# Two fused transformer blocks on one core: new places in SBUF for the matmul operands, and value projections 512 columns wide

## Chip, cores and metric

One core of a Trainium2 chip runs the whole program in one launch. The metric is device microseconds (us) of that core, the median of three runs.

## What is computed

A sequence of 256 tokens with 1,024 features passes a first block (two layers, each a mixer and a squared-ReLU MLP) and a second block (a gated recurrence beside an attention, then a gated FFN). Cut to its skeleton:

```python
def first_block(x, ...):
    for i in range(2):
        hn = rms_norm(x, norm_mix[i])
        mix = even_mixer(hn, ...) if i % 2 == 0 else odd_mixer(hn, ...)
        x = x + mix
        x = x + square(relu(rms_norm(x, norm_mlp[i]) @ w1[i])) @ w2[i]
    return rms_norm(x, norm_final)

def odd_mixer(hn, w_in, w_out, bias_table):
    q, k, v = split(hn @ w_in, 3)
    return moba_attention(q, k, v, bias) @ w_out

def second_block(x, ...):
    xa, ga, q, k, v, f, g_a, g_b = split(rms_norm(x) @ w_in)
    y_a = gelu(ga) * rg_lru(conv(xa)); y_b = forgetting_attention(q, k, v, f)
    x = x + rms_norm((sigmoid(g_a) * (y_a @ w_a) + sigmoid(g_b) * (y_b @ w_b)) @ w_out)
    return x + rms_norm((gelu(gate) * val) @ w_down)      # gate, val = conv(rms_norm(x) @ w_up)
```

All data are 32-bit. The second layer's `v` and the second block's `v` are the two value projections that the change touches (1,024 x 1,024 each).

## The kernel before

Activations stand feature-major: `x`, `gh`, `gl` are tiles of 128 partitions x 8 feature tiles x 256 tokens. For precision every product of an activation with a weight is three products of rounded 32-bit parts: the activation is split into `gh` (rounded) and `gl` (the rest), a weight into `whi` and `wlo`, and `mm3` (L262 to L264) issues whi x gh, whi x gl, wlo x gh into one PSUM bank. Each has a weight load of 128 columns (LDWEIGHTS) and a moving operand of 256 tokens; the load of one matmul runs beside the matmul before it. The same three lines work on other moving tiles:

- `hh`, `hl`: the MLP's hidden features (32 tiles; `hh2`, `hl2` with 24 in the FFN), the "down" stages
- `yh`, `yl`: the recurrence's output
- `oh`, `ol`: the attention's output (`oh1` in the second layer, `oh2` in the second block)

Weights come as a stream (the list `chunks`, `w_load`, `w_split`): a DMA from SyncE brings 1 MB into one of three `raw` buffers, and for each half of it (a unit: 8 x 128, 4 x 256 or 5 x 128 columns) ScalarE casts 128 x 1,024 into `whi` (L220) and VectorE subtracts into `wlo` (L221). There are six buffers of each, and `w_next` keeps up to four units split ahead of TensorE. The program's order is written by hand: generators (`gen_pair`, `gen_nat`, `gen_deep`, `gen_half`) issue a few matmuls at a time, and `Pend.step` and `tick` issue the evacuations in between; `weave` interleaves them with the steps of an attention or of the recurrence.

The value projections are the one place where the roles are turned: `gen_nat` (L435 to L437) makes the activation the loaded operand, and the weights (256 columns of a unit) the moving one, so that the values come out token-major. It takes two units, goes through the eight feature tiles for the first 128 tokens, then for the other 128, and `evac_nat` (L844) scales two halves of 256 columns into `vn`. It is called with n = 4 for the second layer and the second block, and with n = 1 three times in the first layer.

Tiles have no given addresses. Each pool hands out its tiles in the order in which they are asked for, and pools lie one behind the other, so a tile's place follows from the sizes of those ahead of it. In the built program the places (byte within a partition, rest after division by 512) are those of the table in the section on the change. All steps from one feature tile to the next are 512 or 1,024 bytes, so in these stages every matmul of a stage has the same rest for its moving operand and the same for its weights. Two products of the first projections are the exception: the gate logits of the first layer (24 columns) and the forget logits of the second block (16 columns), `gen_small`, whose loaded weights are packed at steps of 96 and 64 bytes.

Of the kernel before, what the change touches and what calls it, by code (L numbers as in the profile page):

```python
# [58 lines left out]
def kernel(  # L59
# [31 lines left out]
    np_ = ctx.enter_context(tc.tile_pool(name="np", bufs=2))  # L91
    rawp = ctx.enter_context(tc.tile_pool(name="rawp", bufs=3))
# [38 lines left out]
    U4 = [(4, 256), (4, 256)]  # L131
    U5 = [(5, 128), (5, 128)]
# [17 lines left out]
    for i in range(4):  # L150
        chunks.append((w_od[i], UA, False))
# [9 lines left out]
    for i in range(10, 14):  # L161
        chunks.append((w_in2[i], UA, False))
# [9 lines left out]

    W = Ctl()
# [56 lines left out]
    # orders of k for a start on two pairs at once: unit by unit for a few k, or k by k  # L230
# [66 lines left out]
    class Norm:  # L297
        # sums of squares over the features; the last `tail` tiles go straight to the summing products
# [263 lines left out]
    def maps_gen(maps, ap):  # L562
# [5 lines left out]
        def A(n):  # L568
            if n % 2 == 0:
                # two heads side by side, on the upper and the lower rows of the array  # L570
                qs = []
                for i in (n, n + 1):
                    m = maps[i]
                    if m.get("pre"):
                        m["pre"]()
                    st[i] = pss.tile([128, 512], F32, tag="s", name="s")
                    qs.append((st[i], m["q"](), m["k"]()))
                for s, q, k in qs:
                    nc.tensor.matmul(out=s[:, 128:384], lhsT=q[:, 128:256], rhs=k, start=True, stop=True)  # L579
# [12 lines left out]
            st[n] = [p, sm, nm]  # L592
# [102 lines left out]
    tb_t = cp.tile([33, 16], F32, name="tb_t")  # L695
# [3 lines left out]
    warm = cp.tile([128, 8], F32, name="warm")  # L699
    nc.scalar.activation(out=warm, in_=mhalf, func=AF.Square)  # L700
    # the tensor engine's clock rises with use: keep it busy until the first weights are here
# [98 lines left out]
    wcmp = [ap0.tile([128, 2048], F32, tag="e8", name="wcmp%d" % i, bufs=2) for i in range(2)]  # L800
# [93 lines left out]
    def compress_gen():  # L894
# [17 lines left out]
        # keys on rows 0..29, values on rows 64..93  # L912
# [38 lines left out]
    # position n of the head order (i, g) -> head g * 4 + i  # L951
# [128 lines left out]
    # the first sums of squares, in tiles that are free so far  # L1080
# [9 lines left out]
    sgain = cp.tile([128, 1], F32, name="sgain")  # L1090
# [60 lines left out]
    def mlp(norm, gain_next, nrm, nrm2=None):  # L1151
        st = ExitStack()
        hp = st.enter_context(tc.tile_pool(name="hp", bufs=1))
        hh = hp.tile([128, 32, T], FR, name="hh")
# [15 lines left out]
    mlp(norm, lambda j: V("mix1", j), nrm)  # L1170
    norm = nrm

    def log1pe(pool, z, n, pre):
        # log(1 + exp(-|z|)) by 2 atanh(e / (2 + e)); returns the steps and the result
# [29 lines left out]
    A1 = ExitStack()  # L1204
    ap1 = A1.enter_context(tc.tile_pool(name="a1", bufs=1))
    rb8 = ap1.tile([128, T], F32, name="rb8")
    vn = ap1.tile([128, 2, D], F32, name="vn")
    oh = ap1.tile([128, KT, T], FR, name="oh1")
    ol = ap1.tile([128, KT, T], FR, name="ol1")
# [11 lines left out]
    def evac_v1(j, ps):  # L1221
        if j == 0:
            nc.vector.tensor_scalar(out=rb8, in0=norm.rb, scalar1=0.125, scalar2=None, op0=ALU.mult)
        evac_nat(vn)(j, ps)
# [30 lines left out]
    run(gen_nat(4, gh, gl, evac_v1, pend))  # L1255
# [12 lines left out]
    nsp = cp.tile([128, 10], F32, name="nsp")  # L1268
    psp = cp.tile([128, 10], F32, name="psp")
    hb = cp.tile([128, 20], F32, name="hb")  # L1270
    hm = cp.tile([128, 16], F32, name="hm")
# [21 lines left out]
    gc = cp.tile([128, 8], F32, name="gc")  # L1293
    nc.vector.tensor_tensor(out=gc, in0=V("fin"), in1=V("pre2"), op=ALU.mult)
    nA, nB = Norm(), Norm()
    mlp(norm, lambda j: gc[:, j:j + 1], nA, nB)

    M = ExitStack()
    mp = M.enter_context(tc.tile_pool(name="mp", bufs=1))
    yh = mp.tile([128, 10, T], FR, name="yh")  # L1300
# [98 lines left out]
    def rg_gen():  # L1399
        for half in range(2):  # L1400
# [5 lines left out]
            for o in range(5):  # L1406
# [3 lines left out]
                for m in range(2):  # L1410
                    # blocks off the diagonal reach at most half of the columns
# [33 lines left out]
    def evac_f(ps):  # L1445
# [14 lines left out]
        def st15():  # L1460
            # log_sigmoid(z) = min(z, 0) - log(1 + exp(-|z|))
# [12 lines left out]
    def evac_gate2(dst, hof):  # L1474
# [12 lines left out]
        gen_nat(4, gh, gl, evac_nat(vn), pend),  # L1487
# [236 lines left out]
def _nats(cols):  # L1724
# [3 lines left out]
    return [[(0, 4, cols[i:i + 256]), (4, 4, cols[i:i + 256])] for i in range(0, len(cols), 256)]  # L1728

# [57 lines left out]
def _prepare(I):  # L1787
# [77 lines left out]
    groups = _nats(ar(2048, 3072))  # L1865
# [8 lines left out]
    groups += _nats(ar(ov, ov + 1024))  # L1874
# [53 lines left out]
```

## Time and profile before

| | before |
|---|---|
| median of three runs | 1175.63 us (1173.75 to 1175.65) |
| profiled execution, first to last instruction (span) | 1170.4 us |
| around the span (median less span) | 5.2 us |
| TensorE matmul busy | 1138.5 us, 97% of the span |
| VectorE, ScalarE, GpSimd busy | 793.4, 625.7, 190.3 us |
| mean granted TensorE clock | 0.993 of 2.4 GHz |

PE is the matmul, PEld the weight load beside it, DVE VectorE, ACT ScalarE, POOL GpSimd. The profiled execution is known by its span; its own time is taken as the span and the 5.2 us around it. Matmuls overlap in the pipeline and each record is some 0.28 us long, so a matmul's duration is not its price: the price is the pace, the time from one start to the next. It is read from a stretch in which TensorE never rests, as its length divided by its matmuls; two that began just ahead of the stretch are counted in it and are taken off.

### The profile page before, as it was taken

How to read it: one execution, taken by the hardware profiler on the slowest of the kernel's cores; microseconds unless marked ns; L12 is line 12 of the kernel's file. 1: busy time of each engine (PE TensorE's matmuls, PEld its weight loads, DVE VectorE, ACT ScalarE, POOL GpSimd, SP SyncE). 2: the span in 40 equal slices, each digit the busy share in tenths (PEclk: the TensorE clock that was granted, in tenths of full speed). 3: DMA queues.
4: the chain of work that ended last, by engine and by line, in shares of the span. 5: the costliest groups of instructions: out<-in, count | busy, mean ns of one | idle time of the engine just before them, and what ended most of it. 6: DMA issues, size and time to landing. Idle time of an engine off the chain costs nothing.

```text
span 1170.4 us, 22694 instructions
## 1 busy us (share of the span) xinstructions
PE 1138.5 (97%) x9343; PEld 1088.1 (93%) x9343; DVE 793.4 (68%) x1404; ACT 625.7 (53%) x1112; POOL 190.3 (16%) x228
## 2 busy tenths in 40 slices
PE   8999999999999999999999999999999999999996
PEld 7987799999999889999999897999999999999996
DVE  5767766674545777566445787766567689999842
ACT  4346555653444545565434577644454556676641
POOL 2014320000010123000001000042310123222211
PEclk9999999999999999999999999999999989999998
DMA  8832244555444334355455453564555525445641
GB/s 331 290 136 73 74 180 145 212 202 199 177 184 180 141 113 145 144 214 206 158 215 198 153 204 109 175 239 141 166 180 197 173 99 167 164 175 180 212 149 36
DMA packets 31303, 200.01 MB, mean 171 GB/s; under 512 B 3594, under 2 KB 6042, under 8 KB 9056
## 3 DMA queue, kind: packets, MB, share of 16 engines
q1 hardware_dynamic: 28832, 187.23, 44.6%
q0 software_dynamic: 2080, 11.08, 2.9%
q8 instruction: 73, 1.20, 0.4%
q14 instruction: 30, 0.25, 0.1%
q10 hardware_dynamic: 288, 0.26, 0.1%
HBM read 197.43 MB, written 3.22 MB: 171 GB/s over the span
## 4 chain that ended last, share of the span: by engine, by line
PE 78%; DVE 14%; ACT 3%; issue 2%; POOL 2%; DMA 1%; SPq 0%; POOLq 0%; ACTq 0%
PE g L262 22%; PE g L264 21%; PE g L263 21%; DVE y L1643 4%; DVE wlo L221 4%; PE rgp L1414 2%; PE g L435 2%; PE g L436 2%; PE g L437 2%; PE pt L623 1%; PE o L673 1%; DVE u L1631 1%; ACT whi L220 1%; PE s L579 1%; DVE y L1655 1%
## 5 line engine op out<-in xcount | busy, mean ns | idle before, releaser
L221 DVE TENSOR_TENSOR wlo<-raw,whi 128x1024 fp32r<-128x1024 f32 (+2 forms) x356 | 420.3, 1212 | 114.2 <-ACT whi L220 113.9
L262 PE MATMUL g<-gh,whi 128*128 128x256 f32 x1632 | 463.7, 284 | 3.2 <-ACT whi L220 1.7
L264 PE MATMUL g<-gh,wlo 128*128 128x256 f32 x1632 | 460.1, 282 | 3.1 <-DVE wlo L221 3.1
L263 PE MATMUL g<-gl,whi 128*128 128x256 f32 x1632 | 457.6, 280 | 0.5 <-DVE gl L257 0.4
L220 ACT CAST whi<-raw 128x1024 fp32r<-128x1024 f32 (+2 forms) x356 | 349.9, 1024 | 18.0 <-PE g L263 8.4
L262 PEld LDWEIGHTS g<-gh,whi 128*128 128x128 f32 x1632 | 309.1, 189 | 10.6 <-issue 5.4
L264 PEld LDWEIGHTS g<-gh,wlo 128*128 128x128 f32 x1632 | 309.2, 189 | 7.2 <-DVE wlo L221 7.1
L263 PEld LDWEIGHTS g<-gl,whi 128*128 128x128 f32 x1632 | 309.4, 190 | 1.1 <-DVE gl L257 0.7
L262 PE MATMUL g<-hh,whi 128*128 128x256 f32 x704 | 199.4, 283 | 1.3 <-DVE u L1631 1.3
L264 PE MATMUL g<-hh,wlo 128*128 128x256 f32 x704 | 199.3, 283 | 0.2 <-DVE wlo L221 0.2
L263 PE MATMUL g<-hl,whi 128*128 128x256 f32 x704 | 199.2, 283 | 0.0
L262 PEld LDWEIGHTS g<-hh,whi 128*128 128x128 f32 x704 | 135.1, 192 | 1.5 <-ACT q L1652 1.5
L264 PEld LDWEIGHTS g<-hh,wlo 128*128 128x128 f32 x704 | 135.1, 192 | 0.4 <-DVE wlo L221 0.4
L263 PEld LDWEIGHTS g<-hl,whi 128*128 128x128 f32 x704 | 135.1, 192 | 0.0
L317 POOL TENSOR_TENSOR acc<-acc,sq 128x256 f32<-128x256 f32 x53 | 42.4, 806 | 465.2 <-ACT sq L313 464.3
L612 POOL TENSOR_TENSOR p<-p,rr 128x384 f32<-128x384 f32 x56 | 50.1, 895 | 205.9 <-DVE rr L607 92.8
L597 ACT ACTIVATE p<-p,nm 128x256 f32<-128x256 f32 x112 | 49.9, 448 | 56.0 <-DVE nm L588 55.8
L1643 DVE SCALAR_TENSOR_TENSOR y<-u,cw,y 128x255 f32<-128x255 f32 (+1 forms) x96 | 60.1, 685 | 0.0
L262 PE MATMUL g<-oh,whi 128*128 128x256 f32 x192 | 55.6, 290 | 0.0
L264 PE MATMUL g<-oh,wlo 128*128 128x256 f32 x192 | 54.3, 283 | 0.0
L263 PE MATMUL g<-ol,whi 128*128 128x256 f32 x192 | 54.2, 282 | 0.0
L1160 ACT ACTIVATE u<-u 128x512 f32<-128x512 f32 x32 | 20.2, 632 | 61.9 <-DVE u L1159 61.9
(317 smaller groups left out, 1455.8 us busy)
## 6 DMA issues: line engine op xcount, KB each, us to landing
raw<-in_w_in_dram SPq DMA_DIRECT2D x30, 1024.0 KB, 4.9
raw<-in_w_up_dram SPq DMA_DIRECT2D x24, 1024.0 KB, 4.9
raw<-in_w_m1a_dram SPq DMA_DIRECT2D x16, 1024.0 KB, 4.8
raw<-in_w_m2a_dram SPq DMA_DIRECT2D x16, 1024.0 KB, 5.0
raw<-in_w_m1b_dram SPq DMA_DIRECT2D x16, 1024.0 KB, 4.9
raw<-in_w_m2b_dram SPq DMA_DIRECT2D x16, 1024.0 KB, 4.9
raw<-in_w_od_dram SPq DMA_DIRECT2D x12, 1024.0 KB, 4.8
raw<-in_w_dn_dram SPq DMA_DIRECT2D x12, 1024.0 KB, 4.8
```

The source lines that it names most:

```text
L220: nc.scalar.copy(out=hi[:, a:b], in_=t[:, off + a:off + b])
L221: nc.vector.tensor_tensor(out=lo[:, a:b], in0=t[:, off + a:off + b], in1=hi[:, a:b].bitcast(F32), op=ALU.subtract)
L262: nc.tensor.matmul(out=o, lhsT=wh, rhs=xh, start=start, stop=False, skip_group_check=skip)
L263: nc.tensor.matmul(out=o, lhsT=wh, rhs=xl, start=False, stop=False, skip_group_check=skip)
L264: nc.tensor.matmul(out=o, lhsT=wl, rhs=xh, start=False, stop=stop, skip_group_check=skip)
L317: nc.gpsimd.tensor_tensor(out=self.acc, in0=self.acc, in1=dst, op=ALU.add)
L435: nc.tensor.matmul(out=ps[:, b, :], lhsT=xh[:, k, bs], rhs=wh[:, k % 4, :], start=(k == 0), stop=False)
L436: nc.tensor.matmul(out=ps[:, b, :], lhsT=xh[:, k, bs], rhs=wl[:, k % 4, :], start=False, stop=False)
L437: nc.tensor.matmul(out=ps[:, b, :], lhsT=xl[:, k, bs], rhs=wh[:, k % 4, :], start=False, stop=(k == KT - 1))
L597: nc.scalar.activation(out=p[:, c0:c1], in_=p[:, c0:c1], func=AF.Exp, scale=-1.0, bias=nm[:, b:b + 1], accum_out=sm[:, b:b + 1],)
L612: nc.gpsimd.tensor_tensor(out=pv, in0=pv, in1=w, op=ALU.mult)
L1643: nc.vector.scalar_tensor_tensor(out=y[:, a, d:], in0=u[:, a, 0:T - d], scalar=cw[:, w, c:c + 1], in1=y[:, a, d:], op0=ALU.mult, op1=ALU.add)
```

## The change

Unwritten pad tiles are put at the head of pools (sizes in 4-byte words), `wcmp` and the attention outputs move to the head of theirs, and the small tiles of `cp` are asked for at the start, so that the operands of the matmuls come to other places. No instruction is added by that.

| tile | bytes behind a multiple of 512, before | after | moving tile less weights, before | after |
|---|---|---|---|---|
| `whi`, `wlo` (six each) | 320 | 0 | | |
| `gh`, `gl` | 384 | 192 | 64 | 192 |
| `hh`, `hl` of the first MLP | 320 | 160 | 0 | 160 |
| `hh`, `hl` of the second MLP | 320 | 224 | 0 | 224 |
| `hh2`, `hl2` of the FFN | 320 | 96 | 0 | 96 |
| `yh`, `yl` | 320 | 192 | 0 | 192 |
| `oh`, `ol`, first layer | 416 | 192 | 96 | 192 |
| `oh1`, `ol1`, second layer | 320 | 32 | 0 | 32 |
| `oh2`, `ol2`, second block | 320 | 64 | 0 | 64 |
| `raw` (three) | 64 | 384 | | |

The second part: the two value projections with n = 4 become `gen_wide` with n = 2. A unit is now 2 feature tiles x 512 columns, a matmul moves 512 columns into a whole PSUM bank, both halves of the tokens take each unit in turn, and the evacuation is 512 wide.

```diff
+    pad(xp, 32)
     x = xp.tile([128, KT, T], F32, name="x")
+    pad(xp, 48)
     gh = xp.tile([128, KT, T], FR, name="gh")
...
+    U2 = [(2, 512), (2, 512)]
...
-        chunks.append((w_od[i], UA, False))
+        chunks.append((w_od[i], U2, False))
...
+    pad(wp, 96)
     W = Ctl()
...
+    def gen_wide(n, xh, xl, evac, pend):
+
+        for j in range(n):
+            pss_ = [psg.tile([128, 2, T], F32, tag="g", name="g") for _ in range(2)]
+            for u in range(4):
+                wh, wl, (nk, ncol) = w_next()
+                for b in range(2):
+                    bs = slice(b * 128, b * 128 + 128)
+                    o = pss_[b].rearrange("p a t -> p (a t)")
+                    for k in range(2):
+                        kk = 2 * u + k
+                        nc.tensor.matmul(out=o, lhsT=xh[:, kk, bs], rhs=wh[:, k, :], start=(kk == 0), stop=False)
+                        nc.tensor.matmul(out=o, lhsT=xh[:, kk, bs], rhs=wl[:, k, :], start=False, stop=False)
+                        nc.tensor.matmul(out=o, lhsT=xl[:, kk, bs], rhs=wh[:, k, :], start=False, stop=(kk == KT - 1))
+                    if u == 3:
+                        pend.put(lambda j=j, b=b, o=o: evac(j, b, o))
+                    pend.step()
+                    yield
...
+    def evac_wide(dst):
+        def f(j, b, ps):
+            c = j * 512
+            nc.scalar.activation(out=dst[:, b, c:c + 512], in_=ps, func=AF.Copy, scale=norm.rn[:, b:b + 1])
+        return f
...
+    def mlp(norm, gain_next, nrm, nrm2=None, place=48):
...
+        pad(hp, place)
         hh = hp.tile([128, 32, T], FR, name="hh")
...
-    run(gen_nat(4, gh, gl, evac_v1, pend))
+    run(gen_wide(2, gh, gl, evac_v1, pend))
...
+    pad(mp, 48)
     yh = mp.tile([128, 10, T], FR, name="yh")
...
-        gen_nat(4, gh, gl, evac_nat(vn), pend),
+        gen_wide(2, gh, gl, evac_wide(vn), pend),
...
+    pad(ff, 24)
     hh = ff.tile([128, 24, T], FR, name="hh2")
```

The order of the instructions moves only around the two value projections. On TensorE, at the start of the second layer's projection (`g` is the PSUM bank, the numbers tell buffers apart, the last field is the output's size), before:

```order
2447 L264 MATMUL g_3854<-hh_1954,wlo_3856 128x256
2448 L435 MATMUL g_3995<-whi_3885,gh_91 128x256
2449 L436 MATMUL g_3995<-wlo_3886,gh_91 128x256
2450 L437 MATMUL g_3995<-whi_3885,gl_92 128x256
2469 L435 MATMUL g_3995<-whi_3913,gh_91 128x256
2472 L435 MATMUL g_3995<-whi_3885,gh_91 128x256
```

and now:

```order
2447 L282 MATMUL g_3864<-hh_1964,wlo_3866 128x256
2448 L475 MATMUL g_4002<-whi_3895,gh_101 128x512
2449 L476 MATMUL g_4002<-wlo_3896,gh_101 128x512
2450 L477 MATMUL g_4002<-whi_3895,gl_102 128x512
2454 L475 MATMUL g_4003<-whi_3895,gh_101 128x512
2460 L475 MATMUL g_4002<-whi_3923,gh_101 128x512
```

Before, both units of a step were held through all eight feature tiles and one bank; now a unit is used up in twelve matmuls on two banks, and then the next is taken. The program has 8,484 matmuls in place of 8,676. On ScalarE at the same place (casts of units, then the broadcast of the norm, then the evacuations), before:

```order
188 L220 CAST whi<-raw 128x1024 x3
189 L356 ACTIVATE dg<-cs,rn 128x128
190 L364 COPY rb<-nbc 128x256
191 L844 ACTIVATE vn<-g,rn 128x256 x4
192 L220 CAST whi<-raw 128x1024 x2
193 L844 ACTIVATE vn<-g,rn 128x256 x2
```

and now:

```order
188 L238 CAST whi<-raw 128x1024 x2
189 L374 ACTIVATE dg<-cs,rn 128x128
190 L382 COPY rb<-nbc 128x256
191 L238 CAST whi<-raw 128x1024
192 L886 ACTIVATE vn<-g,rn 128x512 x2
193 L238 CAST whi<-raw 128x1024 x4
```

Eight evacuations of 256 columns have become four of 512, in two groups, and a cast stands between the norm's broadcast and the first of them.

## Rows read from the trace of the kernel before

**Rows 1.** The page: busy time by engine, and the chain by engine.

```profile
PE 1138.5 (97%) x9343; PEld 1088.1 (93%) x9343; DVE 793.4 (68%) x1404; ACT 625.7 (53%) x1112; POOL 190.3 (16%) x228
PE 78%; DVE 14%; ACT 3%; issue 2%; POOL 2%; DMA 1%; SPq 0%; POOLq 0%; ACTq 0%
```

**Rows 2.** Stretches inside stages: length, busy time and instructions of each engine.

```profile
core 0: us, PE busy (x) PEld busy (x) DVE busy (x) ACT busy (x) POOL busy (x), PEclk, DMA share, GB/s
184.00:244.00 60.00, 60.00 (x532) 60.00 (x531) 40.91 (x46) 36.27 (x47) 0.00 (x0) 1.00 0.58 204
482.00:545.00 63.00, 63.00 (x538) 63.00 (x537) 43.33 (x48) 37.86 (x48) 0.00 (x0) 1.00 0.56 200
748.00:781.00 33.00, 33.00 (x282) 33.00 (x281) 22.35 (x28) 16.35 (x23) 13.12 (x13) 1.00 0.70 240
246.00:337.00 91.00, 91.00 (x761) 91.00 (x760) 46.90 (x50) 38.32 (x49) 4.45 (x6) 1.00 0.54 199
546.50:637.50 91.00, 91.00 (x761) 91.00 (x760) 45.37 (x49) 41.11 (x56) 8.66 (x12) 1.00 0.52 195
1096.00:1152.00 56.00, 56.00 (x470) 56.00 (x468) 26.18 (x25) 24.99 (x38) 8.22 (x10) 1.00 0.42 151
143.00:155.00 12.00, 12.00 (x103) 12.00 (x102) 9.40 (x14) 7.45 (x13) 0.00 (x0) 1.00 0.48 176
887.60:910.40 22.80, 22.80 (x192) 22.80 (x192) 19.28 (x29) 11.23 (x15) 0.00 (x0) 1.00 0.57 209
```

**Rows 3.** Groups of TensorE by line and shape: count, busy us, mean ns, idle before.

```profile
L263 PE MATMUL g<-gl,whi 128*128 128x256 f32 x1632 | 457.6, 280 | 0.5 <-DVE gl L257 0.4
L263 PE MATMUL g<-hl,whi 128*128 128x256 f32 x704 | 199.2, 283 | 0.0
L263 PE MATMUL g<-ol,whi 128*128 128x256 f32 x192 | 54.2, 282 | 0.0
L263 PE MATMUL g<-yl,whi 128*128 128x256 f32 x80 | 22.6, 282 | 0.0
L437 PE MATMUL g<-whi,gl 128*128 128x256 f32 x176 | 49.2, 280 | 0.0
```

**Rows 4.** Timeline of PE in the 16-column product (start, us), then one load.

```profile
713.39 0.28 PE L264 MATMUL gs<-gh,wlo 128*16 128x256 f32 x1
...
714.52 0.28 PE L262 MATMUL gs<-gh,whi 128*16 128x256 f32 x1
714.52 0.09 PEld L263 LDWEIGHTS gs<-gl,whi 128*16 128x16 f32 x1
```

**Rows 5.** Stretches of two pairs of the FFN's "up" stage.

```profile
1002.10:1008.20 6.10, 5.93 (x50) 5.72 (x50) 6.10 (x11) 4.22 (x7) 1.68 (x2) 1.00 0.49 169
1020.40:1026.50 6.10, 5.72 (x50) 5.52 (x50) 6.10 (x11) 4.22 (x7) 1.68 (x2) 1.00 0.52 176
```

**Rows 6.** A value projection: a stretch of it, and ScalarE's evacuations by shape.

```profile
347.00:360.50 13.50, 13.50 (x117) 13.50 (x117) 5.02 (x5) 6.33 (x11) 0.00 (x0) 1.00 0.31 109
L844 ACT ACTIVATE vn<-g,rn 128x256 f32<-128x256 f32 x8 | 3.4, 473 | 7.6 <-PE g L437 7.6
L1160 ACT ACTIVATE u<-u 128x512 f32<-128x512 f32 x32 | 20.2, 632 | 61.9 <-DVE u L1159 61.9
```

**Rows 7.** What TensorE waited for: us in total, times, longest.

```profile
PE pt L623 <- POOL p L612: 5.4, 7, 1.3
PE g L264 <- DVE wlo L221: 3.3, 18, 0.4
```

**Rows 8.** DMA issues of the weight stream: KB each, median us to landing.

```profile
raw<-in_w_m1a_dram SPq DMA_DIRECT2D x16, 1024.0 KB, 4.8
raw<-in_w_m2a_dram SPq DMA_DIRECT2D x16, 1024.0 KB, 5.0
```

More of the change, by code (lines that the diff above doesn't have):

```diff
@@ L91, with pad @@
     np_ = ctx.enter_context(tc.tile_pool(name="np", bufs=2))
+    pads = []
+    def pad(pool, n):
+        pads.append(0)
+        pool.tile([128, n], F32, tag="pad%d" % len(pads), name="pad", bufs=1)
     rawp = ctx.enter_context(tc.tile_pool(name="rawp", bufs=3))
@@ L103 @@
     mhalf = cp.tile([128, 8], F32, name="mhalf")
+    tb_t = cp.tile([33, 16], F32, name="tb_t")
+    warm = cp.tile([128, 8], F32, name="warm")
+    sgain = cp.tile([128, 1], F32, name="sgain")
+    nsp = cp.tile([128, 10], F32, name="nsp")
+    psp = cp.tile([128, 10], F32, name="psp")
+    hb = cp.tile([128, 20], F32, name="hb")
+    hm = cp.tile([128, 16], F32, name="hm")
+    gc = cp.tile([128, 8], F32, name="gc")
+    pad(xp, 32)
     x = xp.tile([128, KT, T], F32, name="x")
+    pad(xp, 48)
     gh = xp.tile([128, KT, T], FR, name="gh")
@@ L161 @@
     for i in range(10, 14):
-        chunks.append((w_in2[i], UA, False))
+        chunks.append((w_in2[i], U2, False))
     for i in range(14, 26):
@@ L694 @@
     w_load()
-    tb_t = cp.tile([33, 16], F32, name="tb_t")
     nc.vector.memset(tb_t[32:33, :], NEGB)
@@ L698 @@
     nc.vector.memset(mhalf, -0.5)
-    warm = cp.tile([128, 8], F32, name="warm")
     nc.scalar.activation(out=warm, in_=mhalf, func=AF.Square)
@@ L782 @@
     ap0 = A0.enter_context(tc.tile_pool(name="a0", bufs=1))
+    pad(ap0, 48)
+    wcmp = [ap0.tile([128, 2048], F32, tag="e8", name="wcmp%d" % i, bufs=2) for i in range(2)]
     qT = ap0.tile([128, 4, T], F32, name="qT")
@@ L799 @@
     nlam = ap0.tile([128, 1], F32, name="nlam")
-    wcmp = [ap0.tile([128, 2048], F32, tag="e8", name="wcmp%d" % i, bufs=2) for i in range(2)]
     for i in range(2):
@@ L1089 @@
     norm.tail = 3
-    sgain = cp.tile([128, 1], F32, name="sgain")
     have = {}
@@ L1147 @@
     A0.close()
-    def mlp(norm, gain_next, nrm, nrm2=None):
+    def mlp(norm, gain_next, nrm, nrm2=None, place=48):
         st = ExitStack()
         hp = st.enter_context(tc.tile_pool(name="hp", bufs=1))
+        pad(hp, place)
         hh = hp.tile([128, 32, T], FR, name="hh")
@@ L1169 @@
     nrm = Norm()
-    mlp(norm, lambda j: V("mix1", j), nrm)
+    mlp(norm, lambda j: V("mix1", j), nrm, place=40)
     norm = nrm
@@ L1205 @@
     ap1 = A1.enter_context(tc.tile_pool(name="a1", bufs=1))
+    pad(ap1, 8)
+    oh = ap1.tile([128, KT, T], FR, name="oh1")
+    ol = ap1.tile([128, KT, T], FR, name="ol1")
     rb8 = ap1.tile([128, T], F32, name="rb8")
     vn = ap1.tile([128, 2, D], F32, name="vn")
-    oh = ap1.tile([128, KT, T], FR, name="oh1")
-    ol = ap1.tile([128, KT, T], FR, name="ol1")
     qk = {}
@@ L1219, in evac_qk, with evac_v1 @@
         return f
-    def evac_v1(j, ps):
-        if j == 0:
+    def evac_v1(j, b, ps):
+        if j == 0 and b == 0:
             nc.vector.tensor_scalar(out=rb8, in0=norm.rb, scalar1=0.125, scalar2=None, op0=ALU.mult)
-        evac_nat(vn)(j, ps)
+        evac_wide(vn)(j, b, ps)
     def head4_maps(ap, j, bias, qk, vn, oh, ol, hdone):
@@ L1267 @@
     )
[L1268 to L1271, printed above, removed]
     sp_steps, sp_q = log1pe(cp, V("lam"), 10, "sp")
@@ L1290 @@
     bias_ctx.close()
-    gc = cp.tile([128, 8], F32, name="gc")
     nc.vector.tensor_tensor(out=gc, in0=V("fin"), in1=V("pre2"), op=ALU.mult)
     nA, nB = Norm(), Norm()
-    mlp(norm, lambda j: gc[:, j:j + 1], nA, nB)
+    mlp(norm, lambda j: gc[:, j:j + 1], nA, nB, place=56)
     M = ExitStack()
     mp = M.enter_context(tc.tile_pool(name="mp", bufs=1))
+    pad(mp, 48)
     yh = mp.tile([128, 10, T], FR, name="yh")
@@ L1498 @@
     fp = FA.enter_context(tc.tile_pool(name="fp", bufs=1))
+    pad(fp, 96)
     oh = fp.tile([128, KT, T], FR, name="oh2")
@@ L1728, in _nats, with _wides @@
     return [[(0, 4, cols[i:i + 256]), (4, 4, cols[i:i + 256])] for i in range(0, len(cols), 256)]
+def _wides(cols):
+    import numpy as np
+    cols = np.asarray(cols)
+    return [[(k, 2, cols[i:i + 512]), (k + 2, 2, cols[i:i + 512])] for i in range(0, len(cols), 512) for k in (0, 4)]
 def _deep(w, group=1):
@@ L1864, in _prepare @@
     w = I["od_w_in"][0]
-    groups = _nats(ar(2048, 3072))
+    groups = _wides(ar(2048, 3072))
     for j in range(4):
@@ L1873, in _prepare @@
     groups = _pairs(w, oxa, oxa + 1280) + _pairs(w, oga, oga + 1280)
-    groups += _nats(ar(ov, ov + 1024))
+    groups += _wides(ar(ov, ov + 1024))
     groups += _pairs(w, oa, oa + 1024)
```

## The prediction

> **What bounds the kernel now.** The page comes first: TensorE is busy for 97% of the span, and 78% of the chain that ended last is TensorE, 14% VectorE [rows 1]. So the pace of TensorE is the time, except where VectorE holds the chain. The list of waits agrees: the longest sum for which TensorE waited on another engine is 5.4 us, in the attentions, the next 3.3 us [rows 7].
>
> Then the stretches inside stages. All are of matmuls with 128 loaded columns and 256 moving ones, at granted clock 1.00 (the 2.4 GHz level), with TensorE never idle; yet the pace differs. With the two matmuls that reach in taken off:
> - first MLP, "up" (`gh`, gap 64 between moving tile and weights): 60.00 / 530 = 113.2 ns
> - second MLP, "up" (the same tile, the same gap): 63.00 / 536 = 117.5 ns; second block's gates and q, k: 33.00 / 280 = 117.9 ns
> - both "down" stages (`hh`, gap 0): 91.00 / 759 = 119.9 ns, twice; the FFN's: 56.00 / 468 = 119.7 ns
> - first layer's output projection (`oh`, gap 96): 12.00 / 101 = 118.8 ns; second block's (gap 0): 22.80 / 190 = 120.0 ns [rows 2].
>
> The clock, the shape and the instructions are the same, the places are not. The mean of one record tells the same: 280 ns with `gl`, 283 with `hl`, 282 with `ol` and `yl` [rows 3]. Gap 0 always gives 120; gap 64 gives 113 or 117.5, which it keeps for a whole stage. So there are two sorts of cost: one by place, and one by how the stream happened to start.
>
> How low can the pace go? In the product with 16 loaded columns a load lasts 0.09 us and hardly overlaps anything, its places run through gaps from 320 down to 128, and ten starts lie between 713.39 and 714.52: 113 ns [rows 4]. I take 113.2 as the floor for 256 moving columns, wherever the weights lie.
>
> One stage is not TensorE's. In the FFN's "up" stage VectorE is busy 6.10 of 6.10 us for a pair of units, TensorE 5.93 [rows 5]. The second pair shown is the test: TensorE needs only 5.72 there, and the pair takes 6.10 all the same.
>
> **The change, part by part.** The profiled execution has a span of 1170.4 us, 5.2 us under the median of 1175.6; terms are in us of span, and the 5.2 stays.
>
> *`gh` and `gl`, gap 64 to 192.* 3 x 1632 = 4896 matmuls [rows 3], of which 24 pairs x 48 = 1152 are the FFN's "up" stage; there VectorE's 6.10 stays and I cost them at nothing. If that cover were gone (VectorE shorter than 48 x 117.5 ns = 5.64 us) they would count 1152 x 4.3 ns = 5.0. Of the other 3744 no row has gap 192 with full loads. Bounds: 113.2 (the lowest row) and 120.0 (the highest). I take 113.2: the short loads ran at it over gaps on both sides of 192 [rows 4], while the known bad gap is 0. Then the second MLP gives 768 x 4.3 = 3.3; the second block's gates, q and k 576 x 4.7 = 2.7; the first MLP only some 0.7, since three quarters of it stand at 113.2 already; the other 1632, some at either pace, 1632 x 2.7 (taken a little above half of 4.5) = 4.4. Together 11.1.
>
> *`hh` of the two MLPs, gap 0 to 160 and 224.* 1536 matmuls at 119.9. Bounds 113.2 and 120.0 again. These places are no multiples of 64 bytes, and the one tile before that was none either (`oh`, at 416, gap 96) ran at 118.8, nearer to the upper end; but gap 96 is also nearer to 0. I take the middle: 1536 x 3.35 = 5.1.
>
> *`hh2` of the FFN, gap 0 to 96.* The row with gap 96 has 118.8 ± 1.2, one matmul more or less in its window, against 119.7 now: nothing.
>
> *The smaller tiles.* `yh` 0 to 192: 240 x 6.7 = 1.6. First `oh` 96 to 192: 192 x 5.6 = 1.1. `oh1` 0 to 32, the middle: 192 x 3.35 = 0.6. `oh2` 0 to 64, the paces of gap 64, of which 117.5 is the commoner: 192 x 2.5 = 0.5. Together 3.8.
>
> *Values 512 wide.* Away go 384 matmuls at 13.50 / 115 = 117.4 ns [rows 6], 45.1; in come 192. If what lies above 256 columns at 2.4 GHz (106.7 ns) is paid by the instruction, one takes 213.3 + 6.5 = 219.8 ns, all 42.2; if by the column, 226.4 at the floor, 43.5, or 240 at the worst pace, 46.1. I take 43.5, the floor by the column, which lies between: a gain of 1.6, bounds +2.9 and -1.0. Half of the weight loads go too, which run beside the matmuls. The evacuation: 8 x 473 ns = 3.8 of ScalarE becomes 4 x 632 = 2.5 [rows 6], and ScalarE is busy for 6.33 of 13.50 there: off the path. Banks: each round takes two of three, so the second half of the next round needs the first bank free; it has six matmuls of the old round and six of the new, 12 x 226 ns = 2.7, to be read in 0.63, with a cast of about 1 us perhaps ahead. No new wait. As many `Pend.step` calls (16) come at the same spacing, so the norm and the recurrence woven in come as before; a unit is used up in 12 x 226 ns = 2.7 where two took 5.6, so the weight stream keeps its rate.
>
> *Feeding it.* At 113.2 ns 1 MB is used up every 48 x 113.2 = 5.4 us; it lands in 4.8 to 5.0 with three buffers [rows 8], and the stretch from 184 to 244 ran like that without a gap, VectorE at 40.91 and ScalarE at 36.27 of 60 [rows 2]. The new place of `raw` and the pads are costed at nothing: no instruction comes with them.
>
> *What does not arrive.* In the two attentions of the first block and the `yh` stage TensorE waits for others now and then [rows 7]. Their share of the above is 1.1 + 1.1 (first layer, 408 `gh` matmuls), 1.0 + 0.6 (second, 384) and 1.6, 5.4 in all; I take a third as lost, 1.8.
>
> **Sum:** 11.1 + 5.1 + 3.8 + 1.6 - 1.8 = 19.8. Span 1150.6, time **1155.8 us**.
>
> **A rule against it.** Stages that differ in place, not in shape, clock or engine, run at 113.2, 117.5 and 119.9 [rows 2]. The Trainium skill, page SBUF — State Buffer, section "Who interferes with whom", gives TensorE two read ports, one for the moving operand and one for LDWEIGHTS, independent of each other, and says that TensorE never waits on anyone there. By it no place is better than another, and what is left of the sum is the 1.6 of the wide values: 1174. The trace does not bear it out as it stands, since three paces are seen; but two of them at one and the same place show that place is not everything.
>
> **The rivals.**
> - *Places do nothing by themselves* (the case beside that rule): the pace is a matter of how each stage's stream starts, and gap 0 was 120 by chance in every "down" stage. For: 113.2 and 117.5 at gap 64. Against: four stages at gap 0, all within 0.3 ns. Only the wide values count: 1174, 1172.7 to 1176.6. Also the case in which the new gaps win as much as they lose.
> - *All gaps but 0 are free.* `hh` gives its other half (5.1), `hh2` 576 x 6.5 = 3.7, the small tiles 1.4 more, the wide values their bound (1.3 more), and nothing is lost to waits (1.8): 33.1, 1142.5. For: the short loads at 113. Against: 118.8 at gap 96.
> - *Gap 192 is a bad one*, at 119.9 like 0. Its price falls on `gh`: the first MLP loses its good start, 590 x 6.7 + 178 x 2.4 = 4.4; the second 768 x 2.4 = 1.8; gates, q and k 576 x 2.0 = 1.2; the other 1632 x 4.0 = 6.5; the wide values at 239.8 cost 0.9. The FFN stays with VectorE (48 x 119.9 ns = 5.76, under 6.10). 14.8, less a third of the attentions' 3.2: 13.7, time 1189. It decides from a pace of some 116.6 ns on `gh`, its mean now; beyond that the change is slower unless `hh` pays for it. For: nothing measured at 192 with full loads. Against: the short loads there.
>
> **How the numbers follow.** The forecast (1149 to 1163 with its own bounds) has 0.43, all free 0.25, nothing 0.15, bad 0.13, and 0.04 is left for a pace under my floor. The range takes in all free and nothing with their bounds: 1140 to 1178; outside are the bad case and the last. Within 0.2% (2.4 us, about what a measurement of this kernel can tell from no change) falls most of "nothing". Faster: 0.43 + 0.25 + 0.04 + 0.04 = 0.76; same 0.10; slower 0.14.
>
> **What will show it.** Stretches inside the stages of the changed kernel: `gh` right if both MLPs' "up" stages run at 113 to 114 ns (some 89 us from first to last), wrong from 116.6 on; `hh` right at 116 to 117 (89 us for a "down" stage), the all-free case at 113 (87); `hh2` still near 120. The FFN's "up" pairs still 6.10 with VectorE full; if they shorten, VectorE's work depends on place too, which I exclude. The value projections: 96 matmuls each, 220 to 227 ns apart, with no idle TensorE where the second round takes its second bank. The forecast falls if the two MLPs' "up" stages do not share one pace, or if a wait appears that the page before does not list.

## The result, and the profile after

| | before | after |
|---|---|---|
| median, same chip | 1175.64 us (1173.75 to 1175.91, 4 runs) | 1159.42 us (1158.46 to 1160.51, 4 runs) |
| ratio | | 0.9865, 95% interval 0.9851 to 0.9879 |
| span of the profiled execution | 1170.4 us | 1157.9 us (own time 1159.69) |

The change makes the kernel 16.2 us faster. The forecast was 1155.8: right in direction and within its range, 3.6 us too good.

The page of after, the same two lines as [rows 1] (busy time by engine; the chain by engine):

```profile
PE 1120.6 (97%) x9151; PEld 1061.5 (92%) x9151; DVE 792.3 (68%) x1404; ACT 624.4 (54%) x1104; POOL 189.5 (16%) x228
PE 77%; DVE 15%; ACT 3%; issue 2%; POOL 1%; DMA 1%; SPq 0%; POOLq 0%; ACTq 0%; DVEq 0%
```

VectorE's and ScalarE's sums are what they were, to 1.3 us; TensorE's is shorter by 17.9. Nothing else took the chain over.

Stretches of after, the counterparts of [rows 2] in the same order and with the same columns, after them one of the wide values:

```profile
184.00:244.00 60.00, 60.00 (x532) 60.00 (x531) 40.90 (x46) 36.70 (x47) 0.00 (x0) 1.00 0.58 207
478.00:538.00 60.00, 60.00 (x532) 60.00 (x531) 40.93 (x46) 36.45 (x47) 0.00 (x0) 1.00 0.57 206
739.00:771.00 32.00, 32.00 (x280) 31.46 (x279) 23.02 (x29) 17.44 (x25) 11.60 (x13) 1.00 0.70 243
246.00:334.00 88.00, 88.00 (x753) 88.00 (x752) 46.40 (x50) 38.30 (x49) 4.46 (x6) 1.00 0.54 204
541.00:629.00 88.00, 88.00 (x746) 88.00 (x746) 45.65 (x49) 41.12 (x56) 8.62 (x12) 1.00 0.54 202
1083.00:1140.00 57.00, 57.00 (x477) 57.00 (x477) 27.32 (x28) 26.14 (x39) 8.54 (x10) 1.00 0.42 148
142.00:154.00 12.00, 12.00 (x107) 11.92 (x106) 8.60 (x13) 6.95 (x11) 0.00 (x0) 1.00 0.45 175
877.40:899.40 22.00, 22.00 (x189) 22.00 (x188) 18.91 (x29) 11.22 (x15) 0.00 (x0) 1.00 0.58 208
346.00:357.00 11.00, 11.00 (x50) 9.03 (x49) 5.66 (x6) 5.17 (x7) 0.00 (x0) 1.00 0.50 191
```

By the prediction's way of reading them (two off the count):

| stretch | gap before, after | ns before | ns after |
|---|---|---|---|
| first MLP, up | 64, 192 | 113.2 | 60.00 / 530 = 113.2 |
| second MLP, up | 64, 192 | 117.5 | 113.2 |
| gates, q, k | 64, 192 | 117.9 | 32.00 / 278 = 115.1 |
| first MLP, down | 0, 160 | 119.9 | 88.00 / 751 = 117.2 |
| second MLP, down | 0, 224 | 119.9 | 88.00 / 744 = 118.3 |
| FFN, down | 0, 96 | 119.7 | 57.00 / 475 = 120.0 |
| first layer's output | 96, 192 | 118.8 | 12.00 / 105 = 114.3 |
| second block's output | 0, 64 | 120.0 | 22.00 / 187 = 117.6 |
| values, 256 wide, then 512 | 448, 320 | 117.4 | 11.00 / 48 = 229.2 |

Two pairs of the FFN's up stage (as [rows 5]), then TensorE's two largest waits (as [rows 7]):

```profile
1020.50:1026.60 6.10, 5.73 (x49) 5.53 (x49) 6.10 (x10) 4.22 (x7) 1.67 (x2) 1.00 0.51 177
1026.60:1032.70 6.10, 5.74 (x49) 5.54 (x49) 6.10 (x10) 4.22 (x7) 1.68 (x2) 1.00 0.51 168
...
PE g L282 <- DVE wlo L239: 6.2, 19, 0.4
PE pt L660 <- POOL p L649: 4.7, 6, 1.3
```

VectorE still fills the pair's 6.10 us, so that stage is no shorter. TensorE now waits 6.2 us in all for a weight that VectorE splits (`wlo`), where it was 3.3 [rows 7]: 2.9 us of the gained pace are given back, in pieces of 0.4 us at most.

### The profile page after: what moved, and what is told of

It is laid out like the page before. It is cut to its first block, busy times and chain, and to the rows that moved or that the text cites. A ratio compares the mean times of both kernels' runs of the same rounds, so it can differ in the third digit from the quotient of the medians.

```text
span 1157.9 us, 22302 instructions
## 1 busy us (share of the span) xinstructions
PE 1120.6 (97%) x9151; PEld 1061.5 (92%) x9151; DVE 792.3 (68%) x1404; ACT 624.4 (54%) x1104; POOL 189.5 (16%) x228
## 4 chain that ended last, share of the span: by engine, by line
PE 77%; DVE 15%; ACT 3%; issue 2%; POOL 1%; DMA 1%; SPq 0%; POOLq 0%; ACTq 0%; DVEq 0%
PE g L280 21%; PE g L282 20%; PE g L281 20%; DVE y L1684 4%; DVE wlo L239 4%; PE rgp L1453 2%; PE pt L660 1%; PE g L475 1%; PE g L477 1%; PE g L476 1%; PE o L710 1%; DVE u L1672 1%; PE s L616 1%; ACT whi L238 1%; DVE y L1696 1%
## 5 line engine op out<-in xcount | busy, mean ns | idle before, releaser
L239 DVE TENSOR_TENSOR wlo<-raw,whi 128x1024 fp32r<-128x1024 f32 (+2 forms) x356 | 420.7, 1212 | 116.6 <-ACT whi L238 116.5
L280 PEld LDWEIGHTS g<-hh,whi 128*128 128x128 f32 x704 | 132.3, 188 | 1.5 <-ACT q L1693 1.5
L281 PEld LDWEIGHTS g<-hl,whi 128*128 128x128 f32 x704 | 132.4, 188 | 0.0
```

The lines of the kernel that those rows point to most:

```text
L239: nc.vector.tensor_tensor(out=lo[:, a:b], in0=t[:, off + a:off + b], in1=hi[:, a:b].bitcast(F32), op=ALU.subtract)
L280: nc.tensor.matmul(out=o, lhsT=wh, rhs=xh, start=start, stop=False, skip_group_check=skip)
L281: nc.tensor.matmul(out=o, lhsT=wh, rhs=xl, start=False, stop=False, skip_group_check=skip)
```

## The experiments

**Theory.** The pace of a matmul hangs on the distance between its moving tile and its weights, and at some distances also on how its stream started; the values 512 wide add little. **Rivals:** the distance does nothing and each stream falls into a pace by its start; or the wide values carry the gain.

**How the numbers are read.** Where a pace is given to 0.1 ns below, it is the mean from one start to the next over the matmul records of a stage (waits left out) or of a segment (its first ten matmuls left out), worked out from the trace; the stretches show the same more coarsely. A ratio compares a kernel with the kernel before on the same chip. The runs stand on different chips, where the kernel before took 1174.5 to 1175.7 us, so a difference between two edited kernels is given twice: by the medians, and by the ratios times 1175 us.

**1. A map of the pace by gap (pace_map).** The whole network is left out: only matmuls in the kernel's order of three, on one large tile `M`, in segments of 72. The gap `d` runs in steps of 32 bytes, in three repeats, and one to four fp32 matmuls stand between two segments (code shortened):

```python
for k in range(8):
    wh, wl = M[:, k*128:k*128+128], M[:, 1024+k*128:1024+k*128+128]
    xh, xl = M[:, MH+d+k*256:MH+d+k*256+256], M[:, ML+d+k*256:ML+d+k*256+256]
    nc.tensor.matmul(out=o, lhsT=wh, rhs=xh, ...)
    nc.tensor.matmul(out=o, lhsT=wh, rhs=xl, ...)
    nc.tensor.matmul(out=o, lhsT=wl, rhs=xh, ...)
```

> Leaves out the whole network: only matmuls of the kernel's shape (128 loaded, 256 moving columns, the three products of mm3) in segments of 72, three for each gap between moving and loaded tile (0 to 480 bytes in steps of 32), then with both tiles moved by 32, 64 and 320 bytes, then 512 moving columns at gaps in steps of 64. Theory A (the pace goes by the gap, and at some gaps also by how the stream started): gap 0 runs at 120 ns in all its segments, gap 64 at 113.3 or 117.8, gap 96 in a repeating pattern of 120 in the mean, gap 160 at 117.3, gap 224 at 118.3, gap 192 at 113.3 or 117.8; the same gap has the same paces wherever both tiles lie. Theory B (only the start of the stream decides): every gap shows 113, 118 and 120 among its segments. Theory C (the place of one tile alone decides, as a tile off a multiple of 64): segments with both tiles moved by 32 run otherwise than those at the same gap unmoved. For 512 columns I expect 225 to 230 ns at gap 64 and 192 and 232 to 240 at 0.

Stretches of 7.5 us in the second repeat, gaps 0, 64, 192, 256, 448 (columns as in the stretches above):

```profile
340.60:348.10 7.50, 7.50 (x65) 7.50 (x64) 0.00 (x0) 0.15 (x1) 0.00 (x0) 1.00 0.01 2
358.30:365.80 7.50, 7.50 (x66) 7.50 (x66) 0.00 (x0) 0.13 (x1) 0.00 (x0) 1.00 0.01 2
394.80:402.30 7.50, 7.50 (x69) 7.50 (x68) 0.00 (x0) 0.11 (x1) 0.00 (x0) 1.00 0.00 0
413.00:420.50 7.50, 7.50 (x65) 7.50 (x65) 0.00 (x0) 0.14 (x1) 0.00 (x0) 1.00 0.01 2
467.20:474.70 7.50, 7.50 (x69) 7.50 (x68) 0.00 (x0) 0.07 (x1) 0.00 (x0) 1.00 0.00 0
```

The mean pace, each within 0.04 ns in all repeats (but the very first segment, at whose start the granted clock was still rising):

| gap | 0 | 32 | 64 | 96 | 128 | 160 | 192 | 224 |
|---|---|---|---|---|---|---|---|---|
| ns | 120.0 | 116.7 | 117.8 | 120.0 | 120.0 | 117.3 | 113.3 | 118.3 |
| gap + 256 | 120.0 | 116.7 | 117.8 | 120.0 | 118.7 | 118.7 | 113.3 | 118.4 |

No other engine does more than a copy between segments, the clock is 1.00 in these stretches, and the pace still goes from 113.3 to 120.0. Moving both tiles together by 32, 64 or 320 bytes left gaps 0, 64 and 96 where they were; only gap 192 gave 117.8 in place of 113.3 at 320 (run 4 takes that up). With 512 moving columns the order is not the expected one; gap 0 is the best and 192 the worst: 226.6 at gap 0 and 256, 228.8 at 64 and 320, 232.5 at 128 and 384, 233.3 at 192 and 448.

One thing this run leaves open. The fp32 matmuls between segments come back in the same order in each repeat, so a repeat shows that the same start gives the same pace, not what another start would give. With the moved tiles, gaps 0, 64, 96 and 192 had four segments each in a repeat; the other gaps had one. That distance counts beside the start rests on this run together with runs 4, 6 and 7.

The changed kernel has the map's values: 117.3 over its 768 matmuls at gap 160, 118.3 at 224, 120.0 at 96, 117.8 at 64, 229.1 for the wide ones at gap 320 (there the activation is loaded, so the gap is 0 less 192, modulo 512). The down stages have the same values to 0.1 ns in the profiled executions of runs 2 and 5, and at gap 0 they stand at 120.0 in all four that have them there (before, and runs 3, 6 and 9): these gaps show one pace, without a draw.

**2. The places without the wide values (places_only).**

```diff
-        chunks.append((w_od[i], U2, False))
+        chunks.append((w_od[i], UA, False))
...
-    run(gen_wide(2, gh, gl, evac_v1, pend))
+    run(gen_nat(4, gh, gl, evac_v1, pend))
```

> The change without its second part: all places as in the change, values by gen_nat in 256 columns as before. Theory (the places carry the gain; in the two traces the value matmuls take 45.4 us before and 44.6 after, and at the new places 384 of 256 columns would take 384 x 116.2 ns = 44.6 too): 1159 to 1161 us. Rival (the wide values carry some 3 us, by fewer weight loads or fewer banks): 1162 to 1164.

1161.59 us (1160.98 to 1163.38, 4 runs), ratio 0.9889 [0.9874, 0.9904]. That lies between the two expectations. The places carry most of the gain; the wide values are worth 2.2 us by the medians and 2.8 by the ratios, with intervals that overlap a little. The records show 0.6 of that: 384 matmuls at 116.2 against 192 at 229.1. What the rest is stays open, but the profiled execution shows one thing that can move a run by as much. The second MLP's up stage, with `gh` in the same place as in the changed kernel:

```profile
478.00:538.00 60.00, 60.00 (x512) 60.00 (x511) 41.35 (x46) 35.21 (x45) 0.00 (x0) 1.00 0.57 201
```

60.00 / 510 = 117.6 ns, where after has 113.2 at the same gap of 192. Run 4 shows why one gap can have two paces.

**3. The wide values at the old places (wide_only).** No pad is written out, and the moved tiles stand where they stood.

```diff
+KEEP = False
...
-        pool.tile([128, n], F32, tag="pad%d" % len(pads), name="pad", bufs=1)
+        if KEEP:
+            pool.tile([128, n], F32, tag="pad%d" % len(pads), name="pad", bufs=1)
```

> The kernel before with the second part alone: no pads, the old places, values 512 wide. Theory: within 1 us of the kernel before, 1174.5 to 1176.5. Rival (the wide values save a fixed part for each instruction, 192 x 6.5 ns = 1.2, and more from halved loads, up to 2.9): 1172 to 1174.

1174.5 us (11 runs), ratio 1.0001 [0.9992, 1.0010]: nothing. At the old places the wide matmuls have gap 448 and stand at 233.2 ns, 44.8 us for the 192, where the narrow ones took 45.1 by the prediction. Five starts from the second layer's projection:

```profile
355.60 0.39 PE L479 MATMUL g<-whi,gl 128*128 128x512 f32 x1
355.83 0.40 PE L477 MATMUL g<-whi,gh 128*128 128x512 f32 x1
356.07 0.39 PE L478 MATMUL g<-wlo,gh 128*128 128x512 f32 x1
356.30 0.40 PE L479 MATMUL g<-whi,gl 128*128 128x512 f32 x1
356.54 0.39 PE L477 MATMUL g<-whi,gh 128*128 128x512 f32 x1
```

So the second half of the change does nothing by itself, and what it gains at the new places comes from where its operands lie there.

**4. One gap, many starts (lock_map).** The same matmuls, twelve segments for each gap and each of two places of the weights, with one to four fp32 matmuls of three widths between segments, so that each starts in another way; then segments with 16 or 64 loaded columns. The edit is shown against run 1:

```diff
-    for g, w0, wide in GAPS:
+    for g, w0, nc_, r_ in GAPS:
...
-            for q in range(1 + n % 4):
-                c = 64 + 32 * (n % 3)
+            for q in range(1 + r_ % 4):
+                c = 64 + 32 * (r_ // 4)
```

> Leaves out the whole network, as the map of paces does: segments of 72 matmuls of 256 columns. Gaps 64, 192 and 448, each with the loaded tile at 0 and at 320 bytes and behind twelve different restarts (one to four fp32 products of 64, 96 or 128 columns); then 16 and 64 loaded columns at gaps 0, 64, 96 and 192. Theory (the gap gives the levels, the restart picks one of two): both 113.3 and 117.8 appear at gap 64, 192 and 448, each kept to the segment's end, more of 113.3 at 192 and 448 than at 64, and no other level; the tile's own place does not matter. Rival (the place of the loaded tile decides between the two): at gap 192 all segments at 0 bytes run at 113.3 and all at 320 bytes at 117.8, whatever the restart. For short loads: if the cost is a collision of the two streams of reads, gap 0 with 16 columns falls below 120; if it is a matter of the moving tile alone, it stays at 120.

Two starts at gap 64, then two at gap 192, then two starts of 16 loaded columns at gap 0:

```profile
33.50:41.00 7.50, 7.50 (x66) 7.50 (x65) 0.00 (x0) 0.21 (x1) 0.00 (x0) 1.00 0.01 2
42.60:50.10 7.50, 7.50 (x68) 7.50 (x68) 0.00 (x0) 0.21 (x1) 0.00 (x0) 1.00 0.00 0
232.10:239.60 7.50, 7.50 (x66) 7.50 (x66) 0.00 (x0) 0.21 (x1) 0.00 (x0) 1.00 0.01 2
240.80:248.30 7.50, 7.50 (x68) 7.50 (x68) 0.23 (x1) 0.21 (x1) 0.00 (x0) 1.00 0.00 0
656.00:663.50 7.50, 7.50 (x65) 5.92 (x64) 0.00 (x0) 0.21 (x1) 0.00 (x0) 1.00 0.01 2
665.10:672.60 7.50, 7.50 (x69) 6.22 (x67) 0.00 (x0) 0.19 (x1) 0.00 (x0) 1.00 0.00 0
```

With 128 loaded columns, gaps 64, 192 and 448 have the same two paces, 113.3 and 117.8, and a segment keeps the one that it starts in to its end. What the gap sets is how often the quicker one comes: 2 of 24 starts at gap 64, 16 of 24 at 192, 17 of 24 at 448. The same starts give the same pace with the weights at 0 and at 320 in all but three of 36 pairs, so it is the start that draws, not the weights' own place. "Draws" does not mean at random: at gap 192 the same four of the twelve starts gave the slower pace at both places.

The traces of the kernels show the same. Take every run of 36 or more `gh` matmuls without an interval of over 135 ns: in each of the nine kernel traces there are 40, and every one stands at one of the two paces from end to end; none changes on the way. At gap 64 the quicker pace has 5 of the 40 in the execution that the prediction rested on, and 2 in run 9; at gap 192 it has 30 in after, and at 448 it has 20 in run 8.

Short loads draw too, two starts each: 16 columns at gap 0 ran at 120.0 after one start, at 113.3 after the other. With 64 columns gap 0 gave 113.3 twice and gap 192 gave 119.0 twice, so the order of the gaps is that of 128 loaded columns and no other. The question put to the short loads, whether gap 0 falls below 120, has so no single answer.

**5. Only `gh`, `gl` back at gap 64 (gh_64).**

```diff
+    pad(np_, 32)
...
-    pad(xp, 48)
+    pad(xp, 16)
```

> The change with gh and gl back at a gap of 64 (moved by 128 bytes), all else as in the change. Theory (gap 64 falls mostly into the slower of its two paces, 117.8, gap 192 mostly into 113.3; the FFN's up stage, bound by VectorE, hides 1152 of the 4896 matmuls): between 7 and 12 us more than the change, 1166 to 1172. Rival (gh gains little and the rest carries the change): under 1163. In its trace the FFN's up pairs stay at 6.10 us.

1168.41 us (1165.37 to 1172.3, 6 runs), ratio 0.9948 [0.9928, 0.9967]. `gh`'s place is worth 9.0 us by the medians and 9.8 by the ratios, more than half of the gain. Its runs lie 7 us apart and after's 2; the kernel before, also at gap 64, lies 2 to 6 apart in its batches of runs, so the spread alone shows little. The up stages in its profiled execution (the highest of the six):

```profile
184.00:244.00 60.00, 60.00 (x511) 59.96 (x510) 41.94 (x47) 34.67 (x44) 0.00 (x0) 1.00 0.55 197
478.00:538.00 60.00, 60.00 (x511) 59.97 (x510) 40.89 (x46) 36.01 (x47) 0.00 (x0) 1.00 0.54 188
```

60.00 / 509 = 117.9 in both. The wide values go with it to 233.3, so some 0.8 of the 9.0 (192 x 4.2) are theirs. The FFN's up pairs stay at 6.10 us with VectorE busy for all of it, as in after.

**6. Only the MLPs' `hh`, `hl` back at gap 0 (hh_0).**

```diff
-    mlp(norm, lambda j: V("mix1", j), nrm, place=40)
+    mlp(norm, lambda j: V("mix1", j), nrm, place=128)
...
-    mlp(norm, lambda j: gc[:, j:j + 1], nA, nB, place=56)
+    mlp(norm, lambda j: gc[:, j:j + 1], nA, nB, place=128)
```

> The change with the hidden tiles of both MLPs back at gap 0. Theory (768 matmuls go from 117.3 to 120.0 and 768 from 118.3 to 120.0, all on the path): 2.1 + 1.3 = 3.4 us more than the change, 1162.0 to 1163.6. Rival (the new places of hh give nothing or twice that): 1159 or 1166. Its down stages at 120.0 ns in every matmul.

1163.63 us (1162.76 to 1165.06, 5 runs), ratio 0.9902 [0.9887, 0.9918]: 4.2 us for `hh` by the medians, 4.3 by the ratios, just above what was expected. Both down stages are back at 88.00 / 733 = 120.1 and 88.00 / 734 = 119.9:

```profile
246.00:334.00 88.00, 88.00 (x735) 88.00 (x735) 46.77 (x50) 38.29 (x49) 4.43 (x6) 1.00 0.51 194
541.00:629.00 88.00, 88.00 (x736) 88.00 (x736) 46.40 (x50) 41.89 (x57) 8.62 (x12) 1.00 0.49 186
```

**7. Every large moving tile at gap 192 (all_192).** The change leaves `hh`, `hh2`, `oh1`, `oh2` at 160, 224, 96, 32 and 64.

```diff
-    mlp(norm, lambda j: V("mix1", j), nrm, place=40)
+    mlp(norm, lambda j: V("mix1", j), nrm, place=48)
...
-    pad(ap1, 8)
+    pad(ap1, 48)
...
-    mlp(norm, lambda j: gc[:, j:j + 1], nA, nB, place=56)
+    mlp(norm, lambda j: gc[:, j:j + 1], nA, nB, place=48)
...
-    pad(fp, 96)
...
-    pad(ff, 24)
+    pad(ff, 48)
```

> The change with every streamed tile 192 bytes behind the weights: hh of both MLPs, hh2, oh1 and oh2 too. Theory (113.3 at gap 192, most stages fall into that pace): hh 768 x 4.0 + 768 x 5.0 = 6.9, hh2 576 x 6.7 = 3.8, oh1 and oh2 192 x 3.6 + 192 x 4.4 = 1.5; together 12.2 less than the change, 1146 to 1150, faster than both kernels. Rival (the restart puts the down stages into the slower pace, 117.8): 1156 to 1160, no better than the change.

1152.74 us (1150.58 to 1154.53, 5 runs), ratio 0.9808 [0.9790, 0.9827]: faster than both kernels, by 6.7 us against after (by the medians and by the ratios alike), where the expectation was 12.2: between the theory and its rival. The two MLPs' down stages and the FFN's:

```profile
246.00:334.00 88.00, 88.00 (x771) 87.74 (x771) 47.84 (x53) 39.24 (x52) 4.43 (x6) 1.00 0.56 214
541.00:629.00 88.00, 88.00 (x779) 88.00 (x778) 47.54 (x53) 41.50 (x58) 11.25 (x16) 1.00 0.56 209
...
1080.00:1135.00 55.00, 55.00 (x486) 55.00 (x486) 24.50 (x23) 24.08 (x36) 7.03 (x9) 1.00 0.41 147
```

The second line is all `hh`: 88.00 / 777 = 113.3. (This kernel is ahead of after by then, so the first stretch ends in the value projection.) The FFN's is 55.00 / 484 = 113.6. By the records the three down stages are together 10.5 us shorter than in after. Some of that is lost elsewhere: in this execution the first layer's output stands at 117.2 where after had 114.4, and the second block's drew 117.8, the slower pace of this gap (run 4). That other executions drew other stages, so that its five runs lie 4 us apart, is likely, and was not looked at.

**8. The same at gap 448 (all_448).** The same pads with 112 words where run 7 has 48.

```diff
-    pad(xp, 48)
+    pad(xp, 112)
...
-    pad(wp, 96)
+    pad(wp, 32)
...
-    pad(ap0, 48)
+    pad(ap0, 112)
...
-    mlp(norm, lambda j: V("mix1", j), nrm, place=40)
+    mlp(norm, lambda j: V("mix1", j), nrm, place=112)
...
```

> The changed kernel with every large streamed tile of fp32r at gap 448 (mod 512), that is 64 bytes ahead of a multiple of 512, where the change has 64 to 224 for most. Theory A, the cost of a place repeats every 256 bytes of distance between weights and streamed tile (the matmul-only map shows 113.34 at 192 and at 448): the down stages run at 113.3 or 117.8 ns per matmul, and the kernel takes what it takes with everything at gap 192, 1150 to 1155 us. Theory B, a whole 512 bytes matters in the kernel, where other tiles and weights of 1024-byte rows are in use: the down stages stand at 116 to 120 ns, neither of the two levels, and the time is 1157 us or more.

1152.88 us (1149.22 to 1154.19, 5 runs), ratio 0.9804 [0.9788, 0.9821], down stages at 113.3 in both MLPs and 113.7 in the FFN: the same as run 7. The second MLP's (the last 7 us lie in the next stage), 88.00 / 776 = 113.4:

```profile
541.00:629.00 88.00, 88.00 (x778) 88.00 (x777) 46.81 (x55) 40.29 (x57) 11.78 (x17) 1.00 0.57 216
```

Between these two gaps, 256 bytes apart, the kernel shows no difference.

**9. The kernel before, once more (before_again).** No edit.

> The kernel before, unchanged, profiled once more. Theory A, streamed tiles at gap 64 run at one of two paces, drawn when a stretch of matmuls starts and kept while it goes on: the profiled execution that the prediction rested on had the first MLP's up stage for the most part at 113.3 ns, so here that stage can stand at 117.8 ns throughout, which over its 768 matmuls is up to 3.4 us more, and the span is 1170.4 to 1174 us, with the execution's own time 1.8 us above its span as in each other run. Theory B, the pace is fixed by the program: the stage runs as it did, span 1170.4 us, and what the medians lie above it is time around the span, some 5 us.

Own time 1177.15 us at a span of 1175.4, 1.8 around it. The same stretch of the first MLP's up stage as the first of [rows 2], in this execution:

```profile
184.00:244.00 60.00, 60.00 (x511) 60.00 (x511) 41.83 (x46) 34.75 (x45) 0.00 (x0) 1.00 0.55 198
```

511 matmuls where there were 532: 117.9 ns, not 113.2, in the same program. The pace was drawn, as theory A has it; the span came out 1.4 us above what it allowed. `gh` as a whole stands at 117.5 here, against 116.6 in the execution that the prediction rested on. Of the 5.0 us between the two spans 2.4 arise in this stage, 1.7 in the second block's first projections (480 matmuls at 117.8 here, at 114.2 there), and some 1.0 ahead of both.

## Why the prediction was right, and where it missed

**Places count, and the rival by which they don't has fallen.** The same down stage stands at 120.0 ns with `hh` at gap 0 (run 6), at 117.3 at gap 160 (after) and at 113.3 at gap 192 (run 7); runs 1 and 5 show it from other sides. Half of the rival was right: at gaps 64, 192 and 448 the start counts as well. The rule that the rival stood beside is on the Trainium skill's page SBUF — State Buffer, section "Who interferes with whom": independent read ports for the moving operand and for LDWEIGHTS, and a TensorE that never waits. The pace in run 1 does not fit a reading of it by which no place is better than another: 120.0 ns at gap 0 and 113.3 at gap 192, with no other engine doing more than a copy. What in the chip makes the difference no run here shows. The new place of `raw` was not tested by itself.

**`gh`: 11.1 forecast, 9.0 measured (9.8 by the ratios; run 5, with 0.8 of wide values in it).** The direction and most of the size were right, and the FFN's 1152 matmuls were rightly costed at nothing. Three things in the step failed:
- "I take 113.2", as the pace of gap 192. It has two paces, and some stages draw 117.8: `gh` as a whole stands at 114.5 in after. Its support, the short loads that ran at 113 over several gaps [rows 4], was a single start: in run 4 short loads at gap 0 stood at 113.3 after one start and at 120.0 after another. As a floor 113.2 held; as the pace of a gap it did not.
- "the first MLP only some 0.7, since three quarters of it stand at 113.2 already". That was the draw of one execution (run 9). Nor does gap 64 keep its pace "for a whole stage": in that execution the first MLP's up stage began at 117.8 and went over to 113.3 at 183 us, behind an interval of 220 ns.
- "the other 1632, some at either pace", 4.4. The second block's first projections, 480 of them, stood at 114.2 in that execution already, and drew 115.4 in after.

Term by term, as matmuls times the difference in the mean pace, after against the prediction's execution and then against run 9: second MLP 3.1 and 3.2 (forecast 3.3); gates, q and k 2.0 and 2.0 (2.7); first MLP 0.9 and 3.4 (0.7); the other 1632 1.1 and 2.8 (4.4). That is 7.1 or 11.4 in all, by which execution of before one takes.

**The 5.2 us around the span** was a misreading of the same kind: every execution with both numbers has some 1.8. By that the profiled one of before took 1172.2 us, 3.4 less than the median of 1175.6. So the forecast takes gains that were worked out in a quick execution off the time of usual ones. In the first MLP that made the gain too small, while the gains of most other stages were taken too large. The errors have opposite signs, and that the time came within 3.6 us is in part luck.

**`hh`: 5.1 forecast, 4.2 measured (run 6).** "I take the middle", 116.6, was too good: 117.3 and 118.3, which by the records is 768 x 2.7 + 768 x 1.7 = 3.4. The chosen row was read coarsely (the records of that stage give 119.7 at gap 96, not 118.8), and "nearer to 0" pointed the wrong way: in run 1, 96 and 128 are as bad as 0, and 224 is worse than 160.

**`hh2` at gap 96: nothing, as forecast** (120.0). **Smaller tiles, less waits: 2.0 forecast.** No run tested them by themselves. What the medians leave is 16.2 - 9.0 - 4.2 - 2.2 = 0.8, and the ratios leave -1.1; both lie within the uncertainty of those differences. In the records `oh` and `yh` came to 114.4 and 114.8 (113.2 had been taken), `oh1` to 116.9, `oh2` to 117.8, near what was taken for them. The larger wait for the split weight (6.2 against 3.3) can be where some of it went.

**Wide values: 1.6 forecast.** "The floor by the column", 226.4, is near gap 0's value in run 1 (226.6); the change lies at 229.1. Against narrow ones at the same places the records give 0.6. Nothing waited for the second bank: TensorE is busy for 11.00 of 11.00.

**"Gap 192 is a bad one"** (0.13) has fallen: with 128 loaded and 256 moving columns it is, with 448, the best of the sixteen. **"All gaps but 0 are free"** (0.25) has fallen as well: in run 1, 96, 128, 256 and 352 cost what 0 costs. Its time of 1142.5 was not reached even by run 7, where every large moving tile lies at the best gap; there the draw remains.

**The signs that the prediction named.** Both up stages ran at 113.2 ns, as asked, but that too was a draw: in run 2 one of them did not. `hh` (116 to 117 asked) and the wide values (220 to 227) came out just slower than their signs. The FFN's pairs held at 6.10, and no new wait appeared.

## What to carry to other kernels

Where TensorE is the bound, read its pace from one start to the next in each stage, at equal clock and shape; the stages here that differed by some per cent differed in place or in start. For fp32r products with 128 loaded and 256 moving columns, put every moving tile 192 bytes behind (or 64 ahead of) its weights, counted modulo 256: a pad tile does it, and here, with the wide values, it came to 1.9% where the change's mixed gaps came to 1.4%. For other widths measure anew: with 64 loaded or 512 moving columns gap 192 was the worst of those tried. And do not take the pace of one profiled execution for the stage's: look at a second one before a term rests on it.

## What was not expected of the hardware

- The cost of a distance repeats every 256 bytes at most gaps of run 1 (0, 32, 64, 96, 192, 224), and not quite at 128 and 160 (120.0 against 118.7, 117.3 against 118.7). Those segments also differed in their start, so whether distance or start makes that difference is open.
- 113.3 and 117.8 ns are two paces of one and the same stream at gaps 64, 192 and 448; the start draws one and the stream keeps it until it is interrupted. What about the start decides it stays open.
- In run 1 the record of a weight load is 192 ns long at gaps 0 and 256 with 256 moving columns, and 188 or 189 at the other gaps (medians): the one other trace of the distance that was found.
- No matmul of 256 columns settled below 113.3 ns, and 512 columns took 226.6 to 233.3 with another order of the gaps (0 best, 192 worst). The Trainium skill, page TensorE: Matmul & The Clock Gate, section "Wait — 56ns, not 53.3ns?", has N columns at 2.4 GHz plus some 2.5 ns from start to start, which for 256 columns would be an estimated 109 ns; no run here shows that for these operands.
